# A decoder block in fp32r on one core: other places for the transposes of the residual, for its update and for exchanged products

## The chip, the cores and the metric

The kernel runs on one core of a Trainium2 chip. The metric is the device time of one execution in microseconds; the time of a kernel is the median of its runs. The profile comes from one further execution, taken by the hardware profiler.

## What is computed

One layer of a hybrid decoder block over 256 tokens of width 2048, in fp32. In this order: RMSNorm; a combined projection to queries, keys and values of 16 heads and two gates; dilated-window attention and stick-breaking attention; their projections, gated and merged; an output projection, RMSNorm and residual. Then

```python
u = rmsnorm(h, g_ffn_pre)
up = causal_depthwise_conv(u @ w_up, conv_w, conv_b)          # 2048 -> 2 x 5632
gate_ff, value = split(up)
f = (gelu(gate_ff) * value) @ w_down
h = h + rmsnorm(f, g_ffn_post)
e = p @ w_ple_in                                              # 256 -> 2048
h = h + sigmoid(h @ w_ple_gate) * e
```

The change touches one column of the first projection, the first four columns of the up projection and the first four of the ple-gate projection.

## The kernel before

**Weights.** A plan (`_plan`, from L50) lists all weight blocks of 128 x 128 in the order of their use; eight of them make a tile of 128 x 1024, which is loaded as `raw`. ScalarE copies it to `hi` (fp32r, L260) and VectorE forms `lo = raw - hi` (L329). `block()` hands the next block's pair to TensorE.

**Products.** Activations are split in the same way: a tile such as `u` has 256 columns of high part and 256 of low part for each of the 16 blocks `k` of the width. `mul` (L405 to L412) issues a pair for a block: `hi` against all 512 columns (L410), then `lo` against the first 256 (L412). With `turned` the 256-wide product comes first (L409), so that two 256-wide products of neighbouring blocks meet and then two 512-wide ones. `mm` (L448) runs a column of sixteen blocks and takes the number of the block to exchange. `mul_first` (L416) issues 256-wide products only, and holds back those of the low part of the activation (L425). `three_wide` (L769 to L771) serves groups in which the weights are the 512-wide side: x high by w high, x high by w low, x low by w high, so the low part of the activation is needed by the third product.

**First projection.** Seven of the first eight columns run together ("first"); the eighth, `("qk", 0, 7)`, follows alone into the bank `z` (L722).

**First up columns.** The residual after the attention, `hx`, is kept by token in four tiles of 512 columns. `turn_back(n)` (L1342 to L1347) transposes the pair of blocks `2n`, `2n+1` into a bank of PSUM with four TensorE instructions; `split2(n)` makes the high parts on ScalarE (L524) and the low parts on VectorE (L532) into `u2`. Before this loop runs `e_cols`, the first half of the `e` products (L771), inside which pair 0 is transposed; its four banks `pse` are emptied by `keep_e` (L1463, into `es`). The loop (L1490 to L1505) goes over `k` and four columns `c`. Pair 1's transposes go into `ring[0]`, which is `pse[1]`. For k < 4 it uses `mul_first`, from k = 4 `mul`. `apply` (L1396) updates 256 columns of `hx` from the normed product, and `ahead()` prepares one more weight tile. TensorE, ScalarE and VectorE each run their instructions in the order of the code.

**Between.** After two more up columns the norm's factors are computed (`spread`, L1556 to L1568, ends with `dg`) and turned by a product with ones (`mid`, L1574), in the middle of the seventh column.

**Ple-gate columns.** At the end the same is done with the last residual: `e_cols` for the second half (pair 0 transposed inside it), `high3` (ScalarE, L1666), `low3` (VectorE, L1673) into `u3`, `save3` and `keep_e` (copies, L1669 and L1463), `apply` (L1396), `weigh` (VectorE, L1365, gain of the norm), and `ahead()`. The loop (L1687 to L1714) goes over sixteen `k` with two groups of three products each. Two quarters of `hx` come back from memory by `reload` (L1616). At k = 10 and later the operands of four-block sums are formed for the columns after these (`mixture`, L1143 to L1152).

Of the kernel before, what the change touches and what calls it, by code (L numbers as in the profile page):

```python
# [8 lines left out]
F32 = mybir.dt.float32  # L9
# [7 lines left out]
KT = D // 128  # L17
# [12 lines left out]
HEAD = 7  # L30
# [130 lines left out]
def hybrid_block_kernel(ctx: ExitStack, tc: tile.TileContext, head, gx, xt, pT, convp, bias, masks, gains, w, out):  # L161
# [12 lines left out]
    def scope(name, **kw):  # L174
        st = ExitStack()
        return st, st.enter_context(tc.tile_pool(name=name, bufs=1, reuse_waits="tile", **kw))
# [205 lines left out]
    def block(n=1):  # L382

        b = at["block"]
        at["block"] = b + n
        i, c = divmod(b, 8)
        if c == 0:
            tick(i)
        return hi[i][:, c * 128:(c + n) * 128], lo[i][:, c * 128:(c + n) * 128]
# [15 lines left out]
    def mul(ps, rhs, first, last, turned=False):  # L405

        wh, wl = block()
        if turned:
            PE.matmul(ps[:, :T], wl, rhs[:, :T], start=False, stop=False, skip_group_check=True)  # L409
        PE.matmul(ps, wh, rhs, start=first, stop=last, skip_group_check=True)  # L410
        if not turned:
            PE.matmul(ps[:, :T], wl, rhs[:, :T], start=False, stop=last, skip_group_check=True)  # L412
# [30 lines left out]
    def bank():  # L443
        pool, bufs = banks["of"][banks["n"] % len(banks["of"])]
        banks["n"] += 1
        return pool.tile([128, 2 * T], F32, name="mm", bufs=bufs)

    def mm(key, src, fn=mul, ps=None, even=0, turned=None, mid=None):  # L448

        ps = bank() if ps is None else ps
        for n, (_, k, first, last) in enumerate(group(key)):
            if mid and n in mid:
                mid[n]()
            if fn is mul1 or n < even:
                mul1(ps[:, :T], src[:, k], first, last and fn is mul1)
            else:
                mul(ps, src[:, k], first, last, n == turned)
        return ps  # L460
# [41 lines left out]
    u = Rows("u")  # L502
# [116 lines left out]
    pat_sc, pat = scope("pat", space=PSUM)  # L619
    banks["of"] = [(pm1, 4)]  # L620
    pss = [bank() for _ in range(4)]
# [72 lines left out]
    def qk_evac(s, c, ps):  # L694
        def then(sum_to):
            st, r = (Q, Rq) if c < 4 else (K, R)
            n = "q" if c < 4 else "k"
            if s not in st:
                st[s] = (ab.tile([128, 4, T], F32, name=n), ab.tile([128, 2, 640 if c < 4 else 896], F32R, name=n + "s"))
            DVE.tensor_tensor(st[s][0][:, c % 4], sum_to(temp()), r, OP.mult)  # L700

        def split(lo):
            x, xs = (Q if c < 4 else K)[s]
            a, b, o = split_at("q" if c < 4 else "k", c % 4)
            x, to = x[:, c % 4, a:b], [xs[:, i, o:o + b - a] for i in range(2)]
            if lo:
                DVE.tensor_tensor(to[1], x, f(to[0]), OP.subtract)
            else:
                ACT.activation(to[0], x, AF.Copy)
        defer(both(ps, then), (lambda: split(False), lambda: split(True)))  # L710
# [7 lines left out]
    for c, ps in enumerate(pss):  # L718
        qk_evac(0, c, ps)
        if c == 1:  # L720
            flush()
    qk_evac(0, HEAD, mm(("qk", 0, HEAD), u, ps=pat.tile([128, 512], F32, name="z")))  # L722
    defer((lambda: ACT.activation(tri, mk[:, 3], AF.Copy), None))

    pr = bank()
# [279 lines left out]
    for s in range(NS):  # L1005
# [5 lines left out]
        for c in _columns(s) if s else ():  # L1011
            ps = mm(("qk", s, c), u, turned=TURNED.get(("qk", s, c)))
# [158 lines left out]
    for j in range(0, KT, 4):  # L1171
# [9 lines left out]
        else:  # L1181
            ps = [bank() for _ in range(2)]
# [15 lines left out]
        for kind, src in (("ba", yT[:, :NS]), ("bb", yT[:, NS:])):  # L1198
            ps = [bank() for _ in range(2)]
# [140 lines left out]
    turned = {}  # L1340
# [66 lines left out]
    u2 = Rows("u2")  # L1407
# [8 lines left out]
    ps = [bank() for _ in range(2)]  # L1416
# [26 lines left out]
    ps = [bank() for _ in range(2)]  # L1443
# [9 lines left out]
    apply = update(mix, xt_s)  # L1453
    rs = norm(0, lambda t: ps[t], apply)
# [26 lines left out]
    pss = [bank() for _ in range(FIRST)]  # L1481
    SINGLE = 4
# [5 lines left out]
        nc.sync.dma_start(h1[:, :, n * 512:(n + 1) * 512], hx[n])  # L1488

    for c, k, first, last in group("up"):  # L1490
        if c == 0 and k % 2 == 0 and k < KT - 2:
            n = k // 2 + 1
            turn_back(n, ring[(n - 1) % 4])
            split2(n)
            n == 1 and stream_in(3)
            n < 3 and keep_e(n + 1, es)
            n < 6 and apply(rs, 256 * n + 512, 256 * n + 768)
            n == 1 and [weigh(mix, t, 3, rows[3]) for t in range(2)]
            ahead()
            4 <= n < 6 and nc.sync.dma_start(e0[:, :, (n - 4) * 512:(n - 3) * 512], es[:, :, (n - 4) * 512:(n - 3) * 512])  # L1500
            n >= 6 and save(n - 6)
        if k < SINGLE:
            mul_first(pss, c, u2[:, k], first, FIRST if k < SINGLE - 1 else 0)
        else:
            mul(pss[c], u2[:, k], first, last, (c, k) == (1, SINGLE))  # L1505
    at["hold"], at["look"], at["grow"] = False, 2, 1

    ff = keep.tile([128, 2, D], F32, name="ff", tag="acc")
# [73 lines left out]
    for q in range(NQ):  # L1582
        for n in range(max(len(pss), q * 2 * QT), (q + 1) * 2 * QT):
            settle = n in (len(pss), q * 2 * QT)
            ps = mm(keys[n], u2, **SETTLE if settle else {}, mid={7: mid} if n == len(pss) else None)
# [62 lines left out]
        ps = plain(3, {1: lambda: row(1)} if end else {})  # L1648
# [8 lines left out]
    apply = update(ff)  # L1657
    rs = norm(2, last3, apply)
# [5 lines left out]
    def high3(n):  # L1664
        x, to = turned[n].rearrange("p (a b) -> p a b", a=2), u3[:, 2 * n:2 * n + 2]
        ACT.activation(to[:, :, :T], x, AF.Copy)  # L1666
# [4 lines left out]
    def low3(n):  # L1671
        x, to = turned[n].rearrange("p (a b) -> p a b", a=2), u3[:, 2 * n:2 * n + 2]
        DVE.tensor_tensor(to[:, :, T:], x, f(to[:, :, :T]), OP.subtract)  # L1673
# [3 lines left out]

    pse = e_cols(1, lambda n: n == 6 and turn_back(0))
    high3(0)
    low3(0)  # L1680
    apply(rs, 256, 512)
    keep_e(0, ee[:, :, D // 2:])
    save3(0)
    ps = [bank() for _ in range(2)]
    assert next(plan)[0] == ("pg", 0)
    made = []
    for k in range(KT):  # L1687
        if k % 2 and k < KT - 1:
            n = k // 2 + 1
            turn_back(n)  # L1690
            high3(n)
            low3(n)
            n == 1 and reload(3)
            save3(n)
            n < 4 and keep_e(n, ee[:, :, D // 2:])
            n < 7 and apply(rs, 256 * n + 256, 256 * n + 512)
            n < 3 and [weigh(ff, t, n + 1, g3[:, (n + 1) * 512:(n + 2) * 512]) for t in range(2)]
            n == 6 and [stage() for stage in made[0][1:]]
            if n == KT // 2 - 1:
                made.append(mixture(1))  # L1700
                made[1][0]()
            n <= 2 and sum_early(n - 1)
            n in (4, 5) and sum_early(n - 2, ee[:, n - 4, :D // 2])
        if k == 8:
            mixing(PAIRS)
        if k == 10:
            made.append(mixture(0))
            made[0][0]()
        if k % 2 and k < KT - 2:
            ahead()  # L1710
        k == KT - 3 and [stage() for stage in made[1][1:]]
        w2 = block(4)
        for t in range(2):
            three_wide(ps[t], cut(u3, k, t), w2, k == 0, k == KT - 1)  # L1714
# [31 lines left out]
    ps = [bank() for _ in range(2)]  # L1746
# [82 lines left out]
```

## Time and profile before

| what | value |
|---|---|
| median of 3 runs | 1415.88 us (1415.76 to 1417.04) |
| the profiled execution | 1416.29 us |
| its span | 1414.3 us |
| TensorE clock granted | 1.000 |
| instructions | 20630 |

In rows of the timeline stand the start in us from the span's start, the busy time in us, the engine, the line, the operation, what is written and read, and the shape; `x4` means four instructions merged. PE is TensorE, ACT ScalarE, DVE VectorE, SP the queue that issues most transfers. Products of TensorE overlap: one starts before the modelled end of the one ahead, so distances are best taken from start to start. A bracket at the end names the idle time before the instruction and what ended it.

### The profile page before, as it was taken

The page shows a single profiled execution, that of the slowest core. Times are in us where ns is not written, and L with a number is a line of the kernel's source. Part 1 is how long each engine was busy: PE and PEld are TensorE (multiplying, and loading weights), DVE is VectorE, ACT ScalarE, POOL GpSimd, SP SyncE. Part 2 cuts the span into 40 slices and gives each one's busy share as a digit, 9 for nine tenths or more (in the row PEclk, how much of TensorE's full clock was granted, in tenths as well). Part 3 has the DMA queues.
Part 4 walks back from the last instruction along what each step waited for, and adds up shares of the span by engine and source line. Part 5 has one row for each costly group of instructions (what it writes and reads, how often), then busy time and mean ns, then how long its engine had stood idle before and what let it go on. Part 6 is the DMA issues. An engine that isn't in the chain of part 4 may idle for free.

```text
span 1414.3 us, 20630 instructions
## 1 busy us (share of the span) xinstructions
PE 1408.4 (100%) x7325; PEld 1206.0 (85%) x7325; DVE 1215.5 (86%) x1917; ACT 879.0 (62%) x1344; POOL 85.2 (6%) x101
## 2 busy tenths in 40 slices
PE   9999999999999999999999999999999999999998
PEld 8888888888888888898888888888888888888887
DVE  7887976968889899879999788997889978899797
ACT  7676745656656666666666566655566556566573
POOL 0010010011110020000100000000100001000100
PEclk9999999999999999999999999999999999999999
DMA  7776594786986787777866886377873778637775
GB/s 287 284 220 203 179 285 141 238 255 178 304 230 204 269 249 220 288 268 228 253 197 228 266 263 210 98 273 234 263 220 99 254 243 262 221 97 280 245 234 186
DMA packets 102982, 323.78 MB, mean 229 GB/s; under 512 B 11360, under 2 KB 12000, under 8 KB 102880
## 3 DMA queue, kind: packets, MB, share of 16 engines
q1 hardware_dynamic: 89056, 297.30, 60.7%
q0 software_dynamic: 13824, 25.17, 10.5%
q8 instruction: 57, 0.93, 0.3%
q14 instruction: 45, 0.37, 0.1%
HBM read 317.19 MB, written 5.24 MB: 228 GB/s over the span
## 4 chain that ended last, share of the span: by engine, by line
PE 98%; DVE 0%; ACT 0%; DMA 0%; SPq 0%; issue 0%
PE mm L771 42%; PE mm L410 29%; PE mm L412 15%; PE mm L1037 2%; PE mm L1039 2%; PE mm L1038 2%; PE S L771 1%; PE mm L862 1%; PE mm L863 1%; PE mm L864 1%; PE S L410 0%; PE mm L1347 0%; DMA hd<-in_head 0%; PE mm L432 0%; PE mm L431 0%; PE mm L430 0%
## 5 line engine op out<-in xcount | busy, mean ns | idle before, releaser
L329 DVE TENSOR_TENSOR lo<-raw,hi 128x1024 fp32r<-128x1024 f32 (+1 forms) x498 | 571.9, 1165 | 62.5 <-ACT hi L260 57.6
L410 PE MATMUL mm<-u,hi 128*128 128x512 f32 x1796 | 625.0, 392 | 0.0
L260 ACT ACTIVATE hi<-raw 128x1024 fp32r<-128x1024 f32 (+1 forms) x498 | 496.9, 1011 | 156.9 <-DMA raw<-in_w 60.8
L412 PE MATMUL mm<-u,lo 128*128 128x256 f32 x1780 | 498.8, 280 | 0.2 <-DVE lo L329 0.2
L410 PEld LDWEIGHTS mm<-u,hi 128*128 128x128 f32 x1796 | 335.0, 187 | 72.1
L412 PEld LDWEIGHTS mm<-u,lo 128*128 128x128 f32 x1780 | 336.4, 189 | 1.7 <-DVE lo L329 0.8
L771 PE MATMUL mm<-hi,u 128*128 128x512 f32 (+1 forms) x676 | 217.3, 389 | 0.1
L771 PE MATMUL mm<-hi,ft 128*128 128x512 f32 x504 | 162.7, 389 | 0.0
L771 PEld LDWEIGHTS mm<-hi,u 128*128 128x128 f32 x676 | 126.0, 188 | 25.8 <-DVE u L1673 0.9
L771 PE MATMUL mm<-lo,u 128*128 128x512 f32 (+1 forms) x338 | 130.5, 386 | 0.0
L468 ACT ACTIVATE t<-mm 128x256 f32<-128x256 f32 x116 | 44.0, 379 | 124.1 <-PE mm L412 124.0
L771 PEld LDWEIGHTS mm<-hi,ft 128*128 128x128 f32 x504 | 94.6, 188 | 20.0 <-DVE ff L1264 0.4
L301 POOL DMA_DIRECT2D tsum<-in_w x56 | 49.4, 1024 | 865.1 <-DMA tsum<-in_w 318.0
L771 PE MATMUL mm<-lo,ft 128*128 128x512 f32 x252 | 98.4, 391 | 0.0
L471 DVE TENSOR_TENSOR s<-mm,t 128x256 f32<-128x256 f32 x116 | 48.8, 421 | 47.5 <-ACT t L468 47.5
L771 PE MATMUL mm<-hi,mixed 128*128 128x512 f32 x240 | 83.7, 389 | 0.0
L256 ACT ACTIVATE hi<-wsum 128x512 fp32r<-128x512 f32 x84 | 51.6, 630 | 48.5 <-DVE wsum L279 42.8
L771 PEld LDWEIGHTS mm<-lo,u 128*128 128x128 f32 x338 | 63.6, 188 | 12.2 <-DVE lo L329 0.2
L771 PE MATMUL mm<-hi,mg 128*128 128x512 f32 x196 | 62.8, 390 | 0.0
L1525 ACT ACTIVATE cv<-cpad,cw 128x256 f32<-128x256 f32 x88 | 52.5, 596 | 12.4 <-DVE cpad L1520 12.3
L771 PEld LDWEIGHTS mm<-lo,ft 128*128 128x128 f32 x252 | 47.3, 188 | 10.6 <-DVE lo L322 1.0
L301 POOL DMA_DIRECT2D gh<-in_w x36 | 31.9, 1014 | 387.3 <-ACT hi L260 114.2
(362 smaller groups left out, 1789.1 us busy)
## 6 DMA issues: line engine op xcount, KB each, us to landing
raw<-in_w SPq DMA_DIRECT2D x452, 512.0 KB, 4.6
tsum<-in_w POOLq DMA_DIRECT2D x56, 256.0 KB, 6.8
raw<-in_w SPq DMA_DIRECT2D x50, 256.0 KB, 3.0
tsum<-in_w SPq DMA_DIRECT2D x22, 512.0 KB, 4.9
gh<-in_w SPq DMA_DIRECT2D x18, 512.0 KB, 5.8
gh<-in_w POOLq DMA_DIRECT2D x36, 256.0 KB, 7.1
hd<-in_head SPq DMA_DIRECT2D x6, 576.0 KB, 7.7
tsum<-in_w SPq DMA_DIRECT2D x12, 256.0 KB, 7.2
```

Of the source, the lines that this page charges most:

```text
L256: ACT.activation(hi[i][:, n * 512:(n + 1) * 512], x, AF.Copy)
L260: ACT.activation(hi[i][:, a:b], raw[i][:, a:b] if src is None else src, AF.Copy)
L301: nc.gpsimd.dma_start(x, w[stream[i] + 1 - NE][:, 512:], accum_op=OP.add)
L329: DVE.tensor_tensor(lo[i][:, a:b], raw[i][:, a:b] if src is None else src, f(hi[i][:, a:b]), OP.subtract)
L410: PE.matmul(ps, wh, rhs, start=first, stop=last, skip_group_check=True)
L412: PE.matmul(ps[:, :T], wl, rhs[:, :T], start=False, stop=last, skip_group_check=True)
L468: ACT.activation(t1[0], ps[:, T:], AF.Copy)
L471: DVE.tensor_tensor(out, ps[:, :T], t1[0], OP.add)
L771: PE.matmul(ps, x[i], w[j], start=first and n == 0, stop=last and n == 2, skip_group_check=True)
L1037: PE.matmul(ps[t], xh, wh, start=k == 0, stop=False)
L1038: PE.matmul(ps[t], xh, wl, start=False, stop=False)
L1525: ACT.activation(y, c[:, 2:], AF.Identity, scale=cw[:, n, 2:3], bias=cw[:, n, 3:4])
```

## The change

```diff
-    qk_evac(0, HEAD, mm(("qk", 0, HEAD), u, ps=pat.tile([128, 512], F32, name="z")))
+    qk_evac(0, HEAD, mm(("qk", 0, HEAD), u, turned=2, ps=pat.tile([128, 512], F32, name="z")))
...
     for c, k, first, last in group("up"):
-        if c == 0 and k % 2 == 0 and k < KT - 2:
-            n = k // 2 + 1
+        if c == 0 and (k == 1 or k % 2 == 0 and 2 <= k < KT - 2):
+            n = (k + 2) // 2
             turn_back(n, ring[(n - 1) % 4])
             split2(n)
...
-            mul(pss[c], u2[:, k], first, last, (c, k) == (1, SINGLE))
+            mul(pss[c], u2[:, k], first, last, c == 2 and k % 2 == 0 and k < KT - 2)
...
     high3(0)
+    apply(rs, 256, 512)
     low3(0)
-    apply(rs, 256, 512)
...
-        if k % 2 and k < KT - 1:
+        if k % 2 == 0 and k < KT - 2:
             n = k // 2 + 1
             turn_back(n)
             high3(n)
+            n < 7 and apply(rs, 256 * n + 256, 256 * n + 512)
             low3(n)
             n == 1 and reload(3)
             save3(n)
             n < 4 and keep_e(n, ee[:, :, D // 2:])
-            n < 7 and apply(rs, 256 * n + 256, 256 * n + 512)
+        if k % 2 and k < KT - 1:
+            n = k // 2 + 1
             n < 3 and [weigh(ff, t, n + 1, g3[:, (n + 1) * 512:(n + 2) * 512]) for t in range(2)]
             n == 6 and [stage() for stage in made[0][1:]]
```

In the eighth column of the first projection the pair of block 2 is exchanged, where none was. In the first up columns the transposes of pair 1 are issued at k = 1 instead of k = 0, those of pairs 2 to 7 where they were; the exchanged pair was that of block 4 in the second column, and is now that of blocks 4, 6, 8, 10 and 12 in the third column, behind each group of transposes. In the ple-gate columns the transposes of pairs 1 to 7 are issued at k = 0, 2, ..., 12 instead of 1, 3, ..., 13, with their high and low parts and the copies out of the same banks; the update of the residual stands ahead of the low part; weighting, early weight sums, mixtures and the weight tiles made ahead stay where they were, at odd k (the mixture of pair 0 at k = 10).

On TensorE, at the start of the first up columns (`u_4933` and `u_4934` hold the weights of the `e` products, `u_5778` the residual's pair 0; the first row is the end of `e_cols`):

```order
 L771 MATMUL mm<-u_4933,pTs 128x512
-L1347 MATMUL mm<-idf,hx 128x128 x4
 L420 MATMUL mm<-u_5778,hi 128x256
 L421 MATMUL mm<-u_5778,lo 128x256
...
 L420 MATMUL mm<-u_5778,hi 128x256
 L421 MATMUL mm<-u_5778,lo 128x256
+L1347 MATMUL mm<-idf,hx 128x128 x4
 L420 MATMUL mm<-u_5778,hi 128x256
```

The four transposes have moved behind block 0's eight products in the four columns.

On TensorE, at the start of the ple-gate columns, before (`u_12589` and `u_12590` hold weights of the `e` products, `u_13162` the residual's pair 0):

```order
L771 MATMUL mm<-u_12590,pTs 128x512
L771 MATMUL mm<-u_12589,pTs 128x512
L771 MATMUL mm<-hi,u_13162 128x512
L771 MATMUL mm<-lo,u_13162 128x512
L771 MATMUL mm<-hi,u_13162 128x512 x2
L771 MATMUL mm<-lo,u_13162 128x512
L771 MATMUL mm<-hi,u_13162 128x512
L1347 MATMUL mm<-idf,hx 128x128 x4
```

and now:

```order
L771 MATMUL mm<-u_12590,pTs 128x512
L771 MATMUL mm<-u_12589,pTs 128x512
L1347 MATMUL mm<-idf,hx 128x128 x4
L771 MATMUL mm<-hi,u_13162 128x512
L771 MATMUL mm<-lo,u_13162 128x512
```

Pair 1's transposes stand ahead of block 0's six products instead of behind them, and the later groups likewise, two blocks apart.

On VectorE, in the same columns (L1396 updates the residual, L1673 is the low part of a pair, L1365 the weighting, L329 the low part of a weight tile):

```order
 L329 TENSOR_TENSOR lo<-raw,hi 128x1024
+L1396 SCALAR_TENSOR_TENSOR hx<-ff,sm,hx 128x256 x2
 L1673 TENSOR_TENSOR u_13162<-mm,u_13162 128x2x256
 L1396 SCALAR_TENSOR_TENSOR hx<-ff,sm,hx 128x256 x2
-L1673 TENSOR_TENSOR u_13182<-mm,u_13182 128x2x256
+L1673 TENSOR_TENSOR u_13176<-mm,u_13176 128x2x256
+L1365 TENSOR_TENSOR ff<-ff,g_12844 128x512 x2
 L1396 SCALAR_TENSOR_TENSOR hx<-ff,sm,hx 128x256 x2
+L1673 TENSOR_TENSOR u_13210<-mm,u_13210 128x2x256
 L1365 TENSOR_TENSOR ff<-ff,g_12844 128x512 x2
-L1673 TENSOR_TENSOR u_13216<-mm,u_13216 128x2x256
+L329 TENSOR_TENSOR lo<-raw,hi 128x1024
```

Each update now stands ahead of the low part of the pair transposed just before, and the weighting behind it.

## The prediction

> **What bounds the kernel now.** I read the page first: busy time by engine and the chain that ended last.
>
> ```profile
> span 1414.3 us, 20630 instructions
> PE 1408.4 (100%) x7325; PEld 1206.0 (85%) x7325; DVE 1215.5 (86%) x1917; ACT 879.0 (62%) x1344; POOL 85.2 (6%) x101
> ...
> PE 98%; DVE 0%; ACT 0%; DMA 0%; SPq 0%; issue 0%
> ```
>
> TensorE is the bound and almost never stands still, so a change of order can only win two things: the few places where PE stops, and the pace at which products follow each other. The change issues the same products. The profiled execution took 1416.29 us (1.99 us outside its 1414.3 us span), 0.41 us above the median of the three runs shown, 1415.88 us; they scatter from 1415.76 to 1417.04. A measurement here can tell about 0.2%, or 2.8 us, from no change.
>
> The view of waits, narrowed to PE, names one stop near the change:
>
> ```profile
> PE mm L1347 <- ACT es L1463: 0.5, 1, 0.5
> ```
>
> It lies in the first columns of the up projection. The timeline there, PE first, then ScalarE and VectorE (start us, busy us, instruction, idle before it):
>
> ```profile
> 594.64 0.86 PE L771 MATMUL mm<-u,pTs 128*128 128x512 f32 x3
> ...
> 596.00 0.66 PE L1347 MATMUL mm<-idf,hx 128*128 128x128 f32 x4 [0.51 <-ACT es L1463]
> 596.42 0.36 PE L420 MATMUL mm<-u,hi 128*128 128x256 f32 x1
> ...
> 598.89 0.60 PE L1347 MATMUL mm<-idf,hx 128*128 128x128 f32 x4
> 599.24 0.36 PE L420 MATMUL mm<-u,hi 128*128 128x256 f32 x1
> ...
> 603.03 0.48 PE L410 MATMUL mm<-u,hi 128*128 128x512 f32 x1
> ...
> 594.14 0.84 ACT L524 ACTIVATE u<-mm,epsb 128x256 fp32r<-128x256 f32 x2 [0.96 <-PE mm L1347]
> 594.87 1.08 ACT L1463 ACTIVATE es<-mm 128x512 f32<-128x512 f32 x2
> ...
> 600.39 0.88 DVE L532 SCALAR_TENSOR_TENSOR u<-mm,epsb,u 128x256 fp32r<-128x256 f32 x2
> ```
>
> The transposes at 596.00 write into the bank that the second `es` copy empties, at 594.87 + 1.08 = 595.95. Four products of block 0 need none of that and stand behind them in PE's order.
>
> In the ple-gate columns the stops are partly hidden in modelled ends, so I compare starts: the seven groups of transposes there stand a constant amount of work apart (twelve 512-wide products and four transposes).
>
> ```profile
> 1322.88 0.60 PE L1347 MATMUL mm<-idf,hx 128*128 128x128 f32 x4
> 1326.09 0.60 PE L1347 MATMUL mm<-idf,hx 128*128 128x128 f32 x4
> 1329.31 0.60 PE L1347 MATMUL mm<-idf,hx 128*128 128x128 f32 x4
> ...
> 1331.38 0.42 PE L771 MATMUL mm<-lo,u 128*128 128x512 f32 x1
> 1331.90 0.73 PE L771 MATMUL mm<-hi,u 128*128 128x512 f32 x2
> ...
> 1332.93 0.60 PE L1347 MATMUL mm<-idf,hx 128*128 128x128 f32 x4
> 1336.21 0.60 PE L1347 MATMUL mm<-idf,hx 128*128 128x128 f32 x4
> 1339.40 0.60 PE L1347 MATMUL mm<-idf,hx 128*128 128x128 f32 x4
> 1342.69 0.60 PE L1347 MATMUL mm<-idf,hx 128*128 128x128 f32 x4
> ```
>
> The periods are 3.21, 3.22, 3.62, 3.28, 3.19 and 3.29 us. Three are long. The longest holds 1331.38 to 1331.90, where a 512-wide product waits for the low part of the residual on VectorE:
>
> ```profile
> 1328.82 1.28 DVE L1365 TENSOR_TENSOR ff<-ff,g 128x512 f32<-128x512 f32 x2
> 1330.03 1.22 DVE L329 TENSOR_TENSOR lo<-raw,hi 128x1024 fp32r<-128x1024 f32 x1
> 1331.16 0.68 DVE L1673 TENSOR_TENSOR u<-mm,u 128x512 fp32r<-128x512 f32 x1
> 1331.76 0.87 DVE L1396 SCALAR_TENSOR_TENSOR hx<-ff,sm,hx 128x256 f32<-128x256 f32 x2
> ```
>
> L1673 ends at 1331.84, and PE goes on at 1331.90: VectorE had the weighting and a weight tile's low part to do first.
>
> **The change part by part.**
>
> *First up columns.* The transposes of pair 1 move behind the four products of block 0. The last 512-wide product before the stop is the third of the row at 594.64 and starts about 595.10; these follow each other every 0.23 us, so PE could go on at 595.33 instead of 596.00: 0.67 us. The transposes after the stop take 0.42 us to the next product against 0.35 us at 598.89: another 0.07. Together **0.74 us**. The cover is block 0's eight 256-wide products (two in each of the four columns), 0.12 us each, so the transposes are reached at 595.33 + 0.96 = 596.29, after 595.95: margin 0.34 us. Were the copy later by more than that, the rest would come back as a wait. Block 0's high part comes from the L524 row at 594.14, whose first half is out before 595.33. What is late next: the transposes start 0.29 us later, and after the smaller delay at their end everything behind them on ScalarE and VectorE comes some 0.2 us later, while PE comes 0.74 earlier. The tightest consumer is the product at 603.03, fed by L532, which ends at 600.39 + 0.88 = 601.27; that leaves 1.76 - 0.94 = 0.8 us. No new stop.
>
> *Ple-gate columns.* Each transpose group moves one block ahead, so six more 512-wide products run between it and the product that needs it: 6 x 0.227 = 1.36 us more time. The undisturbed period is 3.21, so the six periods hold 19.81 - 19.24 = **0.57 us** of stops, and the question is whether they all go. The transposes need hx updated sooner; therefore its update moves ahead of the low part. The first case: VectorE is idle before block 0's low part, waiting for ScalarE, and the two halves (0.87 us) fit there. The worst case is the stop at 1331.90. Now the group of pair 2 stands where block 2's first product stood, about 1324.7. ScalarE has a weight tile's high part (about 1.06) before its copy (0.60): 1326.4. Then VectorE, start to start: low part 0.61, weighting 1.20, weight tile 1.14, update 0.79, and the low part of pair 3 with 0.69: it ends at about 1330.8. The product that needs it stood at about 1331.6 without the stop; one more group of transposes now stands ahead of it (0.36): 1331.96. Margin 1.1 us, against -0.25 us before. Later periods have no weighting and the mixture's four operations now stand behind the low part. I count the whole 0.57; both ends: 0 (VectorE's total work is unchanged, and in that one period it is 3.74 us against 3.21) and 0.57. I take the upper end since the backlog of 0.53 is less than the 1.36 won. SP's and POOL's order is unchanged.
>
> *Exchanged products.* A column is sixteen pairs of a 512-wide and a 256-wide product. They run at two paces. First the eighth column of the first group, its last pair followed by L727; then a column with an exchange (L409); then one in mid-stretch; last the final sixteen pairs of the first up columns.
>
> ```profile
> 45.44 0.40 PE L410 MATMUL z<-u,hi 128*128 128x512 f32 x1
> 51.10 0.38 PE L727 MATMUL mm<-mk,R 128*128 128x128 f32 x2
> ...
> 80.97 0.47 PE L410 MATMUL mm<-u,hi 128*128 128x512 f32 x1
> 81.75 0.28 PE L409 MATMUL mm<-u,lo 128*128 128x256 f32 x1
> 86.62 0.82 PE L960 MATMUL S<-mk,e 128*128 128x128 f32 x6
> ...
> 106.14 0.39 PE L410 MATMUL mm<-u,hi 128*128 128x512 f32 x1
> 111.69 0.39 PE L410 MATMUL mm<-u,hi 128*128 128x512 f32 x1
> ...
> 616.00 0.48 PE L410 MATMUL mm<-u,hi 128*128 128x512 f32 x1
> 621.74 0.28 PE L430 MATMUL mm<-u,hi 128*128 128x256 f32 x1
> ```
>
> Sixteen pairs take 5.66 us (0.354 a pair), 5.65 with the restart behind transposes and an exchange in them, 5.55 (0.347) settled, 5.74 unsettled behind transposes. So an exchange that takes is worth 5.74 - 5.65 = 0.09 us in the last stretch of the up columns and, with 0.11 won and about 0.03 paid for the exchange, 0.08 in the eighth column. The four shorter stretches hold 32 pairs: at most 32 x 0.007 = 0.22 less 4 x 0.03, so 0.10, and about -0.04 where a stretch was settled already; I take 0.06. Full: 0.23; if none takes, 0. Whether one takes at these places no row shows, and I take two thirds: **0.16 us**.
>
> Here a rule speaks against this part. The Trainium skill, "TensorE: Matmul & The Clock Gate", section "Back-to-back issue gap", gives each warm product its columns at 2.4 GHz plus 2.5 ns: 215.8 and 109.2 ns, 0.325 us a pair, in whatever order. The trace disagrees, with 0.347 and 0.354 for the same pair; by the page this term would be 0 and the sum 1.31.
>
> **Sum:** 0.74 + 0.57 + 0.16 = 1.47 us. The profiled 1416.29 would become 1414.82, and the median 1415.88 becomes **1414.4 us**, 0.10% faster: within 0.2%.
>
> **The rivals.**
>
> *The order of a pair is worth nothing* (0.23). For it: the unsettled stretch from 616.00 follows an exchange in the second column of the same group that did not last. Against it: 81.75 and its 5.65. Then 1.31 is won: 1414.6 us. The Trainium skill's page named above would give the same.
>
> *The settled pace of the first quarter's columns is lost* (0.08). PE now comes 0.74 + 0.11 us sooner to L1574, which needs `dg`:
>
> ```profile
> 633.94 0.48 DVE L1568 TENSOR_SCALAR dg<-idf,sm 128x128 f32<-128x128 f32 x2
> 635.47 0.61 PE L1574 MATMUL mm<-dg,ones 128*128 128x128 f32 x4
> ```
>
> `dg` is done at 634.42; PE would be there at 634.62. If VectorE's chain does not come earlier too, 0.2 us are left, and a wait there may upset the exchange that follows at once. Some 250 pairs up to 722 us at 0.007 cost 1.7 us: 1416.1 us, no gain.
>
> *The ple-gate stops stay* because VectorE's work and not its order made them (0.06): 0.90 won, 1415.0 us.
>
> *Slower* (0.03): the update moved ahead of the low part blocks it. For pair 3 the update writes hx's third quarter, reloaded from memory:
>
> ```profile
> 1320.40 1.19 SPq L1616 DMA_DIRECT2D hx<-h  x2
> DMA to landing us min/median/max: 4.4/6.1/7.7
> ```
>
> In the new order the update stands at VectorE's head at about 1329.4, not 1331.76. A reload issued at 1320.40 lands by 1328.1 at the slowest of these. The low part behind it has 1.1 us to spare, so a landing after 1330.5 starts to cost, and one after 1332.0 costs more than all gains together; at 1335 the time would be 1414.4 + 4.5, about 1419. That takes 14.6 us from issue to landing instead of 7.7.
>
> **How the numbers follow.** My forecast, both stops gone and most exchanges taking, has 0.60; the rivals have 0.23, 0.08, 0.06 and 0.03. Low end: all of the 0.23 and the runs' own scatter, some 0.6: 1413.7. High end: the lost pace, 1416.1; the rivals up to there leave out only the last. Faster by over 0.2% means below 1413.05: 0.04, kept from the forecast's share for a gain that no row shows. Slower by over 0.2% means above 1418.7: 0.02, most of the last rival. Within 0.2%: 0.94.
>
> **What would show it.** Right: the wait of L1347 for `es` is gone from PE's waits; seven transpose groups of the ple-gate columns start 3.2 us apart throughout, and the first stands at about 1321.5 less what was won before; the eighth column takes 5.58 us and the last up stretch 5.65. Wrong: a new wait of PE at L1574, at L771 behind L1673, or at L1347 behind L1396; pairs at 0.354 us between 637 and 722 us; or a span that shrinks by less than 0.9 us with all of these as forecast.

## The result and the profile after

| | before | after |
|---|---|---|
| median of 22 runs each | 1416.44 us (1415.62 to 1418.83) | 1414.76 us (1413.83 to 1415.61) |
| ratio, 95% interval | | 0.9986 [0.9979, 0.9992] |
| profiled execution | 1416.29 us | 1413.83 us |
| its span | 1414.3 us | 1411.9 us |

The changed kernel is 1.7 us faster, between 1.1 and 3.0 us by the interval, and so within the 0.2% that the forecast named. The median of the kernel before is 0.56 us higher here than over the three runs shown earlier, which are among these 22; the ratio is made with all of them.

The page of the changed kernel, its span and its busy times:

```profile
span 1411.9 us, 20630 instructions
PE 1406.7 (100%) x7325; PEld 1206.4 (85%) x7325; DVE 1215.3 (86%) x1917; ACT 879.1 (62%) x1344; POOL 85.2 (6%) x101
```

The instructions are the same in number, and PE is still the bound. Its busy time fell by 1.7 of the span's 2.4 us: most of what went was never printed as idle time, because a stop that is hidden in a modelled end counts as busy. The view of waits for PE now has one line, which the kernel before has too; the wait of L1347 for `es` is gone, and so is one of 0.2 us of L412 for L329, which lay ahead of everything that was changed:

```profile
PE z L628 <- DVE epsb L597: 1.1, 1, 1.1
```

The first up columns of the changed kernel, PE, then ScalarE:

```profile
594.36 0.28 PE L420 MATMUL mm<-u,hi 128*128 128x256 f32 x1
...
595.32 0.60 PE L1347 MATMUL mm<-idf,hx 128*128 128x128 f32 x4
...
593.90 1.08 ACT L1463 ACTIVATE es<-mm 128x512 f32<-128x512 f32 x2
```

Block 0's eight 256-wide products (two in each of the four columns) run from 594.36 to 595.32, and the transposes follow without idle time, 0.34 us after the second copy ended at 593.90 + 1.08 = 594.98. The ple-gate columns, PE, then the tightest place of VectorE:

```profile
1317.87 0.60 PE L1347 MATMUL mm<-idf,hx 128*128 128x128 f32 x4
1319.70 0.60 PE L1347 MATMUL mm<-idf,hx 128*128 128x128 f32 x4
1322.89 0.60 PE L1347 MATMUL mm<-idf,hx 128*128 128x128 f32 x4
1326.10 0.60 PE L1347 MATMUL mm<-idf,hx 128*128 128x128 f32 x4
1329.30 0.60 PE L1347 MATMUL mm<-idf,hx 128*128 128x128 f32 x4
...
1330.20 0.63 PE L771 MATMUL mm<-hi,u 128*128 128x512 f32 x2
...
1332.51 0.60 PE L1347 MATMUL mm<-idf,hx 128*128 128x128 f32 x4
1335.70 0.60 PE L1347 MATMUL mm<-idf,hx 128*128 128x128 f32 x4
1338.91 0.60 PE L1347 MATMUL mm<-idf,hx 128*128 128x128 f32 x4
...
1327.21 0.87 DVE L1396 SCALAR_TENSOR_TENSOR hx<-ff,sm,hx 128x256 f32<-128x256 f32 x2
1328.00 0.68 DVE L1673 TENSOR_TENSOR u<-mm,u 128x512 fp32r<-128x512 f32 x1
```

The periods from the second group on are 3.19, 3.21, 3.20, 3.21, 3.19 and 3.21 us: none is long any more. Pair 1's group, the first that moved, stands at 1319.70. Pair 3's low part ends at 1328.68; the product of block 6 that needs it runs in the row at 1330.20.

The table takes both executions apart by the start times of PE. "ple-gate" goes from the first group of transposes to the end of the sixteen blocks.

| stage | before | after | difference |
|---|---|---|---|
| start to first `z` product | 45.44 | 44.37 | -1.07 |
| eighth column | 5.66 | 5.65 | -0.01 |
| L727 to first transposes of `hx` | 542.41 | 542.52 | +0.11 |
| up, pair 0's transposes to k = 4 | 9.52 | 8.81 | -0.71 |
| up, k = 4 to 15 | 18.71 | 18.71 | 0.00 |
| to ple-gate transposes | 697.94 | 697.81 | -0.13 |
| ple-gate | 27.56 | 26.95 | -0.61 |
| to the last product, and behind it | 67.04 | 67.04 | 0.00 |

The spans differ by 2.42 us, but 1.07 of that lies ahead of everything that was changed. Nine executions with the same code in that first stage, these two and seven of the experiments, took 44.37 to 45.44 us there: before's was among the longest and after's the shortest. About 0.4 of the 1.07 us is the pace of the first group, explained below: its hundred pairs of products took 0.353 us each in the kernel before and 0.350 in the changed kernel, and 0.347 to 0.349 in the other executions. What the change touches gave 0.71 + 0.61 + 0.01 = 1.33 us, and this stands against the 1.68 us between the medians.

### The profile page after: what moved, and what is told of

It is laid out like the page before. It is cut to its first block, busy times and chain, and to the rows that moved or that the text cites. A ratio compares the mean times of both kernels' runs of the same rounds, so it can differ in the third digit from the quotient of the medians.

```text
span 1411.9 us, 20630 instructions
## 1 busy us (share of the span) xinstructions
PE 1406.7 (100%) x7325; PEld 1206.4 (85%) x7325; DVE 1215.3 (86%) x1917; ACT 879.1 (62%) x1344; POOL 85.2 (6%) x101
## 4 chain that ended last, share of the span: by engine, by line
PE 100%; DVE 0%; ACT 0%; issue 0%
PE mm L771 42%; PE mm L410 29%; PE mm L412 15%; PE mm L1037 2%; PE mm L1039 2%; PE mm L1038 2%; PE S L771 1%; PE mm L864 1%; PE mm L863 1%; PE mm L862 1%; PE mm L1347 0%; PE S L410 0%; PE mm L432 0%; PE mm L431 0%; PE mm L430 0%; PE S L875 0%
## 5 line engine op out<-in xcount | busy, mean ns | idle before, releaser
L329 DVE TENSOR_TENSOR lo<-raw,hi 128x1024 fp32r<-128x1024 f32 (+1 forms) x498 | 571.6, 1166 | 64.2 <-ACT hi L260 59.7
L412 PE MATMUL mm<-u,lo 128*128 128x256 f32 x1776 | 497.4, 280 | 0.0
L412 PEld LDWEIGHTS mm<-u,lo 128*128 128x128 f32 x1776 | 335.6, 189 | 1.3 <-DVE lo L329 0.2
```

The lines of the kernel that those rows point to most:

```text
L329: DVE.tensor_tensor(lo[i][:, a:b], raw[i][:, a:b] if src is None else src, f(hi[i][:, a:b]), OP.subtract)
```

## The experiments

A time below is the median of ten or eleven runs (22 for the changed kernel, four for the one without exchanges), beside 1416.34 to 1416.44 us for the kernel before on the same chip. The parts are smaller than the 0.1% to which such a ratio is known, so the stages of the traces decide. With the code of before in them, the two changed stages repeat within 0.03 us from trace to trace (9.52 to 9.54 and 27.56 to 27.59); the long stage between `L727` and the first transposes does not (542.41 to 543.21 with its code unchanged). All in us:

| kernel | up, to k = 4 | up, k = 4 to 15 | ple-gate | median | ratio, 95% interval |
|---|---|---|---|---|---|
| before | 9.52 | 18.71 | 27.56 | | |
| after | 8.81 | 18.71 | 26.95 | 1414.76 | 0.9986 [0.9979, 0.9992] |
| up order alone | 8.81 | 18.68 | 27.59 | 1416.29 | 0.9998 [0.999, 1.0007] |
| ple-gate order alone | 9.52 | 18.71 | 26.96 | 1415.36 | 0.9993 [0.9984, 1.0002] |
| exchanges alone | 9.52 | 18.70 | 27.59 | 1416.30 | 1.0003 [0.9994, 1.0012] |
| no exchanges at all | 9.52 | 18.73 | 27.59 | 1426.40 | 1.0073 [1.0058, 1.0089] |
| copies of `es` in other order | 9.05 | 18.68 | 27.59 | 1416.38 | 1.0001 [0.9991, 1.001] |
| after, updates behind | 8.81 | 18.71 | 28.22 | 1415.82 | 0.9997 [0.9988, 1.0007] |
| after, first update ahead | 8.81 | 18.71 | 27.36 | 1415.16 | 0.9993 [0.9983, 1.0003] |
| update ahead alone | 9.54 | 18.68 | 27.59 | 1416.06 | 1.0 [0.999, 1.0009] |
| after, exchanges elsewhere | 8.81 | 18.65 | 26.95 | 1415.24 | 0.9991 [0.9982, 1.0] |

**The up order alone**, on the kernel before:

```diff
-        if c == 0 and k % 2 == 0 and k < KT - 2:
-            n = k // 2 + 1
+        if c == 0 and (k == 1 or k % 2 == 0 and 2 <= k < KT - 2):
+            n = (k + 2) // 2
```

> Only the transposes of pair 1 move behind block 0 in the first up columns; everything else is as before. Theory (the stop at 596 is the wait for the second copy of the e columns, and block 0's products cover it): the idle of L1347 behind L1463 is gone from PE's waits, the stretch from the last e product to the first exchanged pair shrinks by 0.70 to 0.75 us, and the time falls by about 0.7 us, to 0.9995 of before. Rival (the wait only moves to the low part or the next transposes): a new wait of 0.3 us or more on PE between 596 and 604, and less than 0.4 us won there.

The stage shrank by 0.71 us, as in the changed kernel, and from k = 4 on nothing moved by more than 0.03.

**The ple-gate order alone**: the changed kernel with the first projection and the up columns of before.

```diff
-    qk_evac(0, HEAD, mm(("qk", 0, HEAD), u, turned=2, ps=pat.tile([128, 512], F32, name="z")))
+    qk_evac(0, HEAD, mm(("qk", 0, HEAD), u, ps=pat.tile([128, 512], F32, name="z")))
...
-        if c == 0 and (k == 1 or k % 2 == 0 and 2 <= k < KT - 2):
-            n = (k + 2) // 2
+        if c == 0 and k % 2 == 0 and k < KT - 2:
+            n = k // 2 + 1
...
-            mul(pss[c], u2[:, k], first, last, c == 2 and k % 2 == 0 and k < KT - 2)
+            mul(pss[c], u2[:, k], first, last, (c, k) == (1, SINGLE))
```

> Only the ple-gate columns are changed: transposes one block earlier, update ahead of the low part. Theory (the stops were the distance between a transpose and its use, not VectorE's amount of work): all six periods between the seven groups of transposes are 3.19 to 3.23 us, 19.2 in all instead of 19.8, and the time falls by about 0.6 us, to 0.9996 of before. Rival (VectorE's work is the bound there): at least one period stays over 3.4 us and the sum falls by less than 0.3.

26.96 us against 27.56, period for period as in the changed kernel. The two orders are independent of each other: their gains stand side by side in it.

**The exchanges alone**, on the kernel before:

```diff
-    qk_evac(0, HEAD, mm(("qk", 0, HEAD), u, ps=pat.tile([128, 512], F32, name="z")))
+    qk_evac(0, HEAD, mm(("qk", 0, HEAD), u, turned=2, ps=pat.tile([128, 512], F32, name="z")))
...
-            mul(pss[c], u2[:, k], first, last, (c, k) == (1, SINGLE))
+            mul(pss[c], u2[:, k], first, last, c == 2 and k % 2 == 0 and k < KT - 2)
```

> Only the two exchanges are changed: block 2 of the eighth column, and the third column of the first up group. Theory now, after the trace of the changed kernel (an exchange settles the pace only if the pair ahead of it was the 233 and 117 ns one of the unsettled cycle of three): the eighth column stays at 0.354 us a pair, since the pair ahead is the 236 and 113 ns one; of the five exchanges in the up group four settle their stretch, and 0.05 to 0.15 us are won in all, nothing that the time can show (0.9999). Rival (the prediction's): all settle, 0.23 us; other rival: none, 0.

The eighth column took 5.65 us, the up columns from k = 4 on 18.70 instead of 18.71. The exchanges are worth 0.02 us, less than the 0.05 to 0.15 expected. Why shows in the changed kernel's rows: the eighth column up to its exchange, and its last row with L727; then the last sixteen pairs of the up columns, with the exchange at 615.12 and the next column at 620.06.

```profile
44.37 0.40 PE L410 MATMUL z<-u,hi 128*128 128x512 f32 x1
...
44.73 0.40 PE L410 MATMUL z<-u,hi 128*128 128x512 f32 x1
44.97 0.28 PE L412 MATMUL z<-u,lo 128*128 128x256 f32 x1
45.08 0.28 PE L409 MATMUL z<-u,lo 128*128 128x256 f32 x1
...
50.02 0.38 PE L727 MATMUL mm<-mk,R 128*128 128x128 f32 x2
...
614.32 0.48 PE L410 MATMUL mm<-u,hi 128*128 128x512 f32 x1
...
614.75 0.40 PE L410 MATMUL mm<-u,hi 128*128 128x512 f32 x1
615.00 0.28 PE L412 MATMUL mm<-u,lo 128*128 128x256 f32 x1
615.12 0.28 PE L409 MATMUL mm<-u,lo 128*128 128x256 f32 x1
...
620.06 0.28 PE L430 MATMUL mm<-u,hi 128*128 128x256 f32 x1
```

The unsettled pace is a cycle of three pairs whose two products take 241 and 120, 236 and 113, and 233 and 117 ns from start to start. In the eighth column the pair ahead of the exchange was the second of these (0.24 and 0.11 in the rows), in the last up stretch the first (0.25 and 0.12); behind both the pace stayed that of before, 5.65 and 5.74 us for sixteen pairs. The four exchanges in between, behind pairs of 230 to 233 and 117 or 118 ns, did settle their stretches of eight pairs, to 2.885 to 2.892 us. But the same four take 2.892 (with before's own exchange), 2.905, 2.905 and, in the good pace by itself, 2.855 us in the kernel before: 11.557 us together, and 11.555 after. So three of the four gained 0.002, 0.017 and 0.020 us, and the fourth lost 0.037.

What an exchange does in the eighth column depends on the pace that the column starts with. In the executions above it started unsettled. In one kernel described below, the changed kernel with only the first update ahead, whose first projection is that of the changed kernel, it started settled, and there the added exchange ended the good pace:

```profile
44.52 0.39 PE L410 MATMUL z<-u,hi 128*128 128x512 f32 x1
...
45.21 0.28 PE L409 MATMUL z<-u,lo 128*128 128x256 f32 x1
...
50.16 0.38 PE L727 MATMUL mm<-mk,R 128*128 128x128 f32 x2
```

The two pairs ahead of the exchange take 0.69 us, 0.347 each; behind it the unsettled cycle runs to the end of the column, which takes 5.63 us. Two executions without the exchange that started settled, those of the up order alone and of the ple-gate order alone, took 5.55 us. Here the exchange cost 0.08 us instead of winning it.

**No exchanges at all**, on the kernel before. All exchanged pairs of `mul` are taken out, in the other projections and columns too; the same products in another order:

```diff
-SETTLE = dict(even=8, turned=9)
+SETTLE = dict(even=8)
...
-            mul(pss[c], u[:, k], first, last, (c, k) == (1, 1))
+            mul(pss[c], u[:, k], first, last)
...
-            ps = mm(("qk", s, c), u, turned=TURNED.get(("qk", s, c)))
+            ps = mm(("qk", s, c), u, turned=None)
...
-            mul(pss[c], u2[:, k], first, last, (c, k) == (1, SINGLE))
+            mul(pss[c], u2[:, k], first, last, False)
```

> All exchanged pairs of the kernel before are taken out: in the query and key columns, the up columns, and the first groups; nothing else changes and every product is still issued. Theory (the order of a pair sets the pace of all pairs behind it, 0.354 against 0.347 us): some 1,600 pairs that ran settled run at 0.353 or 0.354, and the time grows by 9 to 11 us, to 1.007 of before; the window from 640 to 720 us takes 0.353 us a pair. Rival (each product costs its columns in any order): no change, within 0.2%.

The span grew by 9.3 us and the time by 0.73% [0.58, 0.89]. From the end of the first up columns to the ple-gate transposes it takes 704.63 instead of 697.94 us, and 2.05 us more between L727 and the first transposes of `hx`. Another 1.07 us lie behind the ple-gate columns, where no such pairs stand, and are not counted for their order. Of some 1350 pairs behind 600 us 362 take 361 ns, the longest of the unsettled cycle, where the changed kernel has 5 of them; with one in each cycle of three, four pairs in five run unsettled. Rows of such a stretch, first and last, in the kernel without exchanges:

```profile
809.76 0.40 PE L410 MATMUL mm<-u,hi 128*128 128x512 f32 x1
...
811.88 0.40 PE L410 MATMUL mm<-u,hi 128*128 128x512 f32 x1
```

and of the changed kernel, which is settled there:

```profile
808.85 0.39 PE L410 MATMUL mm<-u,hi 128*128 128x512 f32 x1
...
810.93 0.39 PE L410 MATMUL mm<-u,hi 128*128 128x512 f32 x1
```

Six pairs lie between the rows of each: 2.12 us without exchanges, 2.08 in the changed kernel, or 0.3533 and 0.3467 us a pair. From 781.46, 960.33 and 1139.21 us on the changed kernel runs 339 pairs in a row at 0.3467 each time; 1017 pairs by 0.0066 are the 6.7 us of this stage.

One part of the expectation was missed. From 640 to 720 us the kernel without exchanges does not take 0.353 us a pair:

```profile
649.79 0.40 PE L410 MATMUL mm<-u,hi 128*128 128x512 f32 x1
...
651.87 0.40 PE L410 MATMUL mm<-u,hi 128*128 128x512 f32 x1
```

These six pairs take 2.08 us, 0.3467 each. In this stretch, which begins behind L1574 and holds some 240 pairs, pairs of 343 and 350 ns alternate, and so the faster pace came without any exchange. An exchange can bring the faster pace, but the pace does not hang on exchanges alone. All in all the order of a pair's two products is worth a great deal in this kernel, but not at the places of this change.

**The copies of `es` in the other order**, on the kernel before: the copy that empties the bank of pair 1's transposes comes first.

```diff
-    for n in range(2):
+    for n in (1, 0):
```

> The kernel before with one exchange on ScalarE: of the two copies of e columns ahead of the first up columns, that of the bank which the transposes of pair 1 need goes first. Theory (the stop at 596 is the wait for that bank and for nothing else): the transposes start about 0.48 us earlier, the stop falls from 0.67 to about 0.19 us, and the stretch up to k = 4 from 9.52 to about 9.05 us. Rival (the transposes would have waited for the updated residual or the low part as well): less than 0.2 us won.

```profile
594.85 1.08 ACT L1463 ACTIVATE es<-mm 128x512 f32<-128x512 f32 x2
...
595.50 0.66 PE L1347 MATMUL mm<-idf,hx 128*128 128x128 f32 x4
```

The transposes start 0.65 us after ScalarE began the copies, against 1.13 us before (594.87 to 596.00): one copy less. The stage fell by 0.47 us. So the stop was the wait for that one bank; 0.24 us of the 0.71 are left with the one copy that still comes first, and the changed kernel hides that behind products.

**The changed kernel with the updates behind the low part**, as before:

```diff
-    apply(rs, 256, 512)
     low3(0)
+    apply(rs, 256, 512)
...
-            n < 7 and apply(rs, 256 * n + 256, 256 * n + 512)
             low3(n)
             n == 1 and reload(3)
             save3(n)
             n < 4 and keep_e(n, ee[:, :, D // 2:])
+            n < 7 and apply(rs, 256 * n + 256, 256 * n + 512)
```

> The changed kernel with the update of the residual back behind the low part, in all ple-gate blocks; the transposes stay one block earlier. Theory (the earlier transposes need the earlier update at one place only, block 0, where the transposes of pair 1 follow at once): L1347 waits for L1396 there by 0.7 to 0.95 us, the first period (from the transposes of pair 0 to those of pair 1) grows by that, all later periods stay at 3.2 us, and the time is that of the changed kernel plus 0.8 us. Rival (the order on VectorE matters nowhere): as the changed kernel. Other rival (it matters in every period): two or more periods of over 3.4 us.

PE has a new wait, and the rows show its place:

```profile
1318.58 0.60 PE L1347 MATMUL mm<-idf,hx 128*128 128x128 f32 x4
...
1320.98 0.94 PE L1347 MATMUL mm<-idf,hx 128*128 128x128 f32 x4 [0.41 <-DVE hx L1396]
1321.68 0.48 PE L771 MATMUL mm<-hi,u 128*128 128x512 f32 x1
...
1319.84 0.69 DVE L1673 TENSOR_TENSOR u<-mm,u 128x512 fp32r<-128x512 f32 x1 [1.04 <-ACT u L1666]
1320.45 0.87 DVE L1396 SCALAR_TENSOR_TENSOR hx<-ff,sm,hx 128x256 f32<-128x256 f32 x2
```

VectorE sits idle for 1.04 us ahead of block 0's low part, and the update that the transposes need comes behind it. The transposes start 2.40 us after pair 0's instead of 1.83, and take 0.70 instead of 0.35 us to the next product: 0.92 us at this place. The later groups lose another 0.19 us, which had not been expected (two periods are 3.34 and 3.25 us), and 0.16 comes behind the last group. The part takes 28.22 us, 1.27 more than in the changed kernel and 0.66 more than before the change. Moving the transposes without the update would have been a loss.

**The changed kernel with only the first update ahead**: in the loop the updates go behind the low part again.

```diff
-            n < 7 and apply(rs, 256 * n + 256, 256 * n + 512)
             low3(n)
             n == 1 and reload(3)
             save3(n)
             n < 4 and keep_e(n, ee[:, :, D // 2:])
+            n < 7 and apply(rs, 256 * n + 256, 256 * n + 512)
```

> The changed kernel with the update behind the low part inside the loop, and ahead of it only before the loop. Theory (only the first update is needed that early): every period between transposes is 3.2 us and the ple-gate columns take as long as in the changed kernel, within 0.05 us. Rival: periods over 3.4 us where VectorE has the weighting, 0.3 us or more in all.

```profile
1329.82 0.77 PE L1347 MATMUL mm<-idf,hx 128*128 128x128 f32 x4
1333.19 0.69 PE L1347 MATMUL mm<-idf,hx 128*128 128x128 f32 x4
1336.49 0.60 PE L1347 MATMUL mm<-idf,hx 128*128 128x128 f32 x4
...
1329.12 0.87 DVE L1396 SCALAR_TENSOR_TENSOR hx<-ff,sm,hx 128x256 f32<-128x256 f32 x2
```

27.36 us, 0.41 more than the changed kernel, where I had expected almost nothing. Of that 0.26 is lost at the transposes of pairs 4 and 5, and the other 0.15 behind the last group. At pair 4's transposes the update they need ends at 1329.12 + 0.87 = 1329.99, they start at 1329.82 and are drawn out to 0.77, and the periods there are 3.37 and 3.30 us. No idle time is printed for it, since the stop lies inside the group of four.

**The update ahead alone**, on the kernel before, with its transposes where they were:

```diff
     high3(0)
+    apply(rs, 256, 512)
     low3(0)
-    apply(rs, 256, 512)
...
             high3(n)
+            n < 7 and apply(rs, 256 * n + 256, 256 * n + 512)
             low3(n)
             n == 1 and reload(3)
             save3(n)
             n < 4 and keep_e(n, ee[:, :, D // 2:])
-            n < 7 and apply(rs, 256 * n + 256, 256 * n + 512)
```

> The kernel before with only the update moved ahead of the low part; transposes at odd blocks as before. Theory (the update fits into VectorE's idle time where there is any, but delays the low part where there is none, and there the low part is due at once): the two stops at the periods of 3.62 and 3.29 us grow, the ple-gate columns take 0.6 to 1.5 us more than before. Rival (the update's place is what removed the stops): they take 0.3 us or more less than before.

Neither the loss nor the small gain came; the part takes 27.59 us, as in other kernels with before's order. The stop of the longest period stays, now with the update ahead of the low part on VectorE:

```profile
1330.53 0.88 DVE L1396 SCALAR_TENSOR_TENSOR hx<-ff,sm,hx 128x256 f32<-128x256 f32 x2
1331.32 0.68 DVE L1673 TENSOR_TENSOR u<-mm,u 128x512 fp32r<-128x512 f32 x1
...
1332.06 0.73 PE L771 MATMUL mm<-hi,u 128*128 128x512 f32 x2 [0.15 <-DVE u L1673]
```

The first update now fills VectorE's idle time ahead of block 0's low part. That idle time shrinks from 1.05 to 0.26 us. So the one update more that stands ahead of every later low part is paid for already, which would explain why nothing is lost. Here L1673 ends at 1332.00 and PE goes on at 1332.06; in the kernel before, whose part began 0.16 us earlier, that was 1331.84 and 1331.90.

**The changed kernel with its exchanges at other places**, chosen by the pair ahead:

```diff
-            mul(pss[c], u[:, k], first, last, (c, k) == (1, 1))
+            mul(pss[c], u[:, k], first, last, c == 1 and k in (1, 9, 10, 11))
...
-    qk_evac(0, HEAD, mm(("qk", 0, HEAD), u, turned=2, ps=pat.tile([128, 512], F32, name="z")))
+    qk_evac(0, HEAD, mm(("qk", 0, HEAD), u, ps=pat.tile([128, 512], F32, name="z")))
...
-            mul(pss[c], u2[:, k], first, last, c == 2 and k % 2 == 0 and k < KT - 2)
+            mul(pss[c], u2[:, k], first, last, c == 2 and k % 2 == 0 and k < KT - 4 or (c, k) == (0, KT - 3))
```

> The changed kernel with its exchanges at other places: in the first group at blocks 1, 9, 10 and 11 of the second column instead of block 1 alone, none in the eighth column, and in the last stretch of the first up columns at block 13 of the first column (behind a pair that took about 233 and 117 ns) instead of block 12 of the third (behind 241 and 120). Theory, that an exchange settles the pace where the pair ahead took 230 to 234 and 117 to 118 ns and fails behind the other two pairs of the unsettled cycle: the last up stretch of sixteen pairs goes from 5.74 to about 5.65 us, the eighth column from 5.65 to 5.55 because the first group ends settled, and at most 0.4 us in all are won against the changed kernel. Rival, that whether an exchange takes is left to chance from execution to execution: the last stretch stays at 5.74 and the eighth column at 5.65, and nothing is won. The transposes' periods in the ple-gate columns stay 3.2 us throughout and the start of the first up columns stays at 8.81 us. Median by the theory about 0.3 us below that of the changed kernel (about 1414.5), which the timing alone cannot tell; the stretches in the trace decide.

Rows of it: the first group from the exchange of block 9 on, then the last up stretch.

```profile
27.77 0.28 PE L409 MATMUL mm<-u,lo 128*128 128x256 f32 x1
...
28.82 0.40 PE L410 MATMUL S<-u,hi 128*128 128x512 f32 x1
...
29.18 0.40 PE L410 MATMUL S<-u,hi 128*128 128x512 f32 x1
...
614.82 0.48 PE L410 MATMUL mm<-u,hi 128*128 128x512 f32 x1
...
615.96 0.40 PE L410 MATMUL mm<-u,hi 128*128 128x512 f32 x1
616.19 0.28 PE L412 MATMUL mm<-u,lo 128*128 128x256 f32 x1
616.31 0.28 PE L409 MATMUL mm<-u,lo 128*128 128x256 f32 x1
...
620.49 0.28 PE L430 MATMUL mm<-u,hi 128*128 128x256 f32 x1
```

The theory held in one half. In the last up stretch the exchange at 616.31 stands behind a pair of 0.23 and 0.12 us, and the sixteen pairs now take 620.49 - 614.82 = 5.67 us instead of 5.74. In the first group the pace was already settled in this execution, 0.347 us a pair from 9.4 to 27.8 us, and the exchange of block 9 itself upset it: behind it the unsettled cycle runs to the end of the group (28.82 to 29.18 is a pair of 0.36). The exchanges of blocks 10 and 11 fell behind pairs of 241 and 120 and did not mend it, and the eighth column stayed at 5.65 us. So this kernel is no better than the changed one. Its profiled span, 1414.2 us, is 2.3 us longer: 0.6 of it ahead of the first `z` product, and 1.67 in the columns behind the ple-gate stage, from 1359 us on, where the view of waits prints one of 0.5 us for the low part of a weight tile. That tile came late: five loads of weight tiles, issued 17.8 to 30.1 us behind the first ple-gate transposes, took 8.8 to 11.8 us to land, where the same five took 6.6 to 9.3 in the changed kernel. Why they were slower no run here shows; the kernels without exchanges and with the copies of `es` swapped lose 1.1 and 0.8 us at the same products.

## Why the prediction was right, point by point

**First up columns, 0.74 us.** Measured 0.71, in the changed kernel and with this part alone. The margin of 0.34 us to the copy came out to the hundredth (595.32 less 594.98). The cover is eight products, as the sum has it, and not the four that its text names beside them. Reordering the copies showed that the wait was for the bank: with one copy less ahead of the transposes 0.47 us went.

**Ple-gate columns, 0.57 us.** Measured 0.61: all the long periods went. The margin at pair 3's low part was 1330.20 - 1328.68 = 1.5 us, where 1.1 had been forecast. The forecast place of the first group that moved, 1321.5 less what was won before it, came out as well: it stands at 1319.70, and the part began 1.81 us earlier. The choice of the upper end rested on the time won for VectorE, six products, and this held; but the experiments add what the sum did not price: the transposes alone would have lost 0.66 us, the update alone gives nothing, and with the update ahead only once 0.41 of the gain goes. The rival in which the stops stay is refuted for this order, and true of the update by itself.

**Exchanged products, 0.16 us.** This term was mis-sized: it measured 0.01 in the eighth column and 0.00 in the up columns, at the end of the range where none takes. (Two thirds of 0.23 are 0.15 and not 0.16, which changes nothing.) The step that failed took two thirds of the full value without asking behind which pair of the cycle each exchange would fall, nor which pace the stretch would have without it. Two of the six stood behind pairs of 236 and 113 and of 241 and 120 ns, and the slower pace went on; the other four brought the faster pace, but three won 0.04 us together and the fourth lost as much, since that stretch had the good pace before. The forecast of 5.58 and 5.65 us for the eighth column and the last up stretch was wrong: 5.65 and 5.74.

**The order of a pair is worth nothing.** For this change the sum came out as that rival's 1.31 has it, but not for its reason. Without exchanges the kernel is 0.73% slower. The Trainium skill, "TensorE: Matmul & The Clock Gate", section "Back-to-back issue gap", gives the distance between products by their width alone, with a formula that it calls the gap of an isolated product. The measured 0.3467 and 0.3533 us for the same pair decide against it here.

**The settled pace of the first quarter lost at L1574.** It was not:

```profile
632.22 0.48 DVE L1568 TENSOR_SCALAR dg<-idf,sm 128x128 f32<-128x128 f32 x2
...
633.79 0.61 PE L1574 MATMUL mm<-dg,ones 128*128 128x128 f32 x4
```

`dg` was done at 632.70, 1.09 us ahead of PE, against 1.05 before: VectorE's chain came forward with PE's. The pairs from 635.66 to 719.90 run at 0.3467 us. And the exchange that stands there is not the only way to this pace: the kernel without any runs the stretch at 0.3467 us too.

**Slower by a late reload.** No update waited for it: the one at 1327.21 started as the operation ahead of it ended.

**The time.** 1414.4 us had been forecast from a median of 1415.88; the kernel before then ran at 1416.44 and the changed one at 1414.76. The trace accounts for 1.33 of the 1.68 us, which the interval of the ratio, 1.1 to 3.0 us, holds as well; for the other 0.35 no stage was found, and stages with unchanged code vary by more than that. That the 1.68 us lie nearer to the forecast 1.47 than the 1.31 us of the first two parts do is therefore no evidence for the third: its 0.16 were not won, and the sum is close by luck in that term.

## What to carry to other kernels

When an instruction is issued earlier in order to give its consumer time, look at what must come earlier with it: here the transposes gained 0.61 us only together with the update that feeds them, and lost 0.66 us without it. An operation that waits on a bank that is just being emptied can stand behind work that needs neither, if that work is longer than the copy. And before a change is judged by the difference of two profiled spans, take them apart by stage: 1.07 of 2.42 us here came ahead of the first changed instruction.

## What was unexpected of the hardware

Pairs of a 512-wide and a 256-wide product settle into one of two paces, 0.3467 or 0.3533 us on average, and stay there for hundreds of products. In these runs a pair with its order exchanged brought the faster pace behind a pair of 233 and 117 ns, or of 230 and 118 shortly behind transposes; the slower pace went on behind 241 and 120 or 236 and 113. In the two cases where it stood in a stretch that was long settled, behind 230 and 116 or 117, it ended the good pace. This rule fits the stretches compared here; as a forecast it was tried at few places, and at one of them, the last up stretch, it came true. The faster pace also came without an exchange, behind L1574 in the kernel that has none. In which pace the first group runs differs between executions. The eighth column took 5.55 us without any exchange in the up order's and the ple-gate order's executions, 5.63 to 5.66 in the others. What in TensorE makes the two paces, no run here shows.
